# A decoder trunk step: 33 of 44 gate/up pairs by a Strassen scheme, with the residual kept in DRAM meanwhile

## The chip, the cores and the metric

The kernel runs on one core of a Trainium2 chip. TensorE (PE) multiplies, VectorE (DVE), ScalarE (ACT) and GpSimd (POOL) work element by element, and SyncE (SP) issues all DMAs of this kernel, in order. The metric is the device time of one execution in microseconds, the median of three runs. "PEld" in the profile is PE's loading of the stationary operand, which overlaps its matmuls.

## The reference

One inference step of a trunk of two layers, for a prompt of 512 tokens and 8 samples of 8 new tokens, which share all weights: 576 rows of 1024 channels. Cut to what matters:

```python
for i in range(DEPTH):                      # 2
    h = rms_norm(x, norm_mix_pre[i])
    m = pool_mixer(h, ...) if i % 2 == 0 else gdn_mixer(h, ...)   # layer 0: pooling; layer 1: gated delta rule
    x = x + rms_norm(m, norm_mix_post[i])
    h = rms_norm(x, norm_ffn_pre[i])
    x = x + rms_norm(swiglu(h, ffn_w_in[i], ffn_w_out[i]), norm_ffn_post[i])

def swiglu(h, w_in, w_out):                 # w_in (1024, 5632), w_out (2816, 1024)
    gu = h @ w_in
    return (jax.nn.silu(gu[..., :D_FF]) * gu[..., D_FF:]) @ w_out
```

All data are float32. The pooling and the delta rule also return their new states.

## The kernel before

**Layout.** Channels lie on the 128 partitions (8 chunks of 128, index `c` or `k`), the 576 rows along the free dimension, in two halves: half 0 of 256 columns, half 1 of 320 (`HALVES`). Half 0's products go through the ring of three PSUM banks "A", half 1's through the three of "B" (`RING`); "n0" and "n1" are one bank each, for norms and transposes.

**Precision.** Every large product is made of float32 values that are split into a high and a low part: `split2` and `Weights.split` copy on ACT (`wh`, `hH`, `aH`) and subtract on DVE or POOL (`wl`, `hL`, `aL`), and `mm3` sums three matmuls for each chunk of 128 contracted channels: high by high, high by low, low by high.

**Feed-forward layers.** 2816 = 22 x 128, so there are 22 pairs of a gate and an up chunk in a layer. `ffn` lists chunks block by block (`FBLOCKS`, of 8, 7 and 7 pairs): for each pair "g" and "u" (8 x 3 matmuls a half each), then 8 output chunks "y" that contract the block's activations. The first chunks (14 in layer 0, 10 in layer 1) run for half 0 and then again for half 1, so that half 1's norm can be finished beside half 0; then each chunk's weights serve both halves; the last 8 output chunks again run half by half, so that half 0's end (`finish0`, `finish1`) lies beside half 1's products. A weight chunk is 512 KB (`wraw`, three buffers), an output chunk of a 7-pair block 448 KB.

**The end.** In layer 1 the residual is transposed beside the feed-forward work into `xT` (`turn_x`). As each of the last outputs `y` comes, `turn_y` scales it and PE transposes it into banks of the other half's ring, one bank for each row piece and four channel chunks; `finish1` then makes the row norms and adds.

**The mixer of layer 1.** The delta rule's first half of the output product is parked in DRAM (`y_d`), its result `og_d` too, and the residual since the end of layer 0 (`x_d`). When the mixer's pools are closed, `y_d` and `x_d` are loaded, and the second half of the output product is added to it by DVE.

**What sets the order.** Nearly all instructions are recorded by `Plan.put`, and issued by `Plan.finish` in an order that a list scheduler chooses: forward passes with estimated durations, in-order engines and the operations' dependences; 40 rounds with randomly stirred priorities; the best is kept. So all of them have the same line, 283 (302 in the change). An operation of `EITHER` may go to DVE or POOL. Where the planner sees PE waiting for long, it puts idle matmuls there (`ps_w<-ones`, line 279; 298 in the change), whose results nobody reads.

Of the kernel before, what the change touches and what calls it, by code (L numbers as in the profile page):

```python
# [20 lines left out]
P = 128  # L21
# [7 lines left out]
HALVES = ((0, 256), (256, 320))  # L29
DFF = 2816  # L30
FBLOCKS = (8, 7, 7)
# [19 lines left out]
class Plan:  # L51
# [22 lines left out]
    def start(self):  # L74
        self.on = True
        self.ops, self.last, self.tags = [], {}, {}
        self.gone, self.ends, self.home, self.after = set(), set(), {}, {}
        self.banks, self.holds = {}, {}

# [57 lines left out]
    @staticmethod  # L137
    def rows(ap):

        n = list(ap.ap)[0][1]  # L140
        return 32 if n <= 32 else 64 if n <= 64 else 128
# [46 lines left out]
    def put(self, method, calls, a, k):  # L188
# [6 lines left out]
        preds = set()  # L195
# [3 lines left out]
        for x, write in [(x, False) for x in ins] + [(x, True) for x in outs]:  # L199
# [5 lines left out]
            log = self.last.setdefault(name, [])  # L205
# [6 lines left out]
            if x.space == SB and (write or not log):  # L212
                preds.update(self.after[self.home[name]])
            if t.tag in self.tags:
# [3 lines left out]
                if write and p >= bufs:  # L218
                    preds.update(q[0] for q, _ in self.last[names[p - bufs]])
            for q, w in log:  # L220
                if (write or w) and q[0] != i and self.meet(r, q[1]):
                    preds.add(q[0])
            log.append(((i, r), write))
# [18 lines left out]
    def close(self, *pools):  # L242

        self.gone |= {t for t, home in self.home.items() if home in pools}
        touched = {q[0] for t in self.gone for q, _ in self.last[t]}
# [253 lines left out]
def hybrid_kernel(  # L499
# [55 lines left out]
    hv = [None, None]  # L555

    def new_h(hi):
        hv[hi] = [hp.tile([P, NC, HALVES[hi][1]], F32R, name="h%s%d" % (x, hi), tag="h%s%d" % (x, hi), bufs=1)
                  for x in "HL"]

    for hi in range(2):
        new_h(hi)
# [4 lines left out]
    y_d = [dp.tile([P, NC, n], F32, name="y_d%d" % o0) for o0, n in HALVES]  # L567
# [105 lines left out]
    def h_of(hi):  # L673
        hi_, lo = hv[hi]
        return lambda k: (hi_[:, k], lo[:, k])
# [6 lines left out]
    def halftile(tp, what, hi, bufs, shape=None):  # L682
        n = HALVES[hi][1]
        return tp.tile(list(shape or (P, n)), F32, name=what, tag="%s%d" % (what, hi), bufs=bufs)

    def add_sq(tp, acc, src, c, hi):

        if c == 0:
            acc.append(halftile(tp, "nacc", hi, 1))
            ACT.activation(acc[0], src, AF.Square)  # L690
        else:
            sq = halftile(tp, "nsq", hi, 2)
# [14 lines left out]
    def rstd(tp, acc, hi, on_dve=False):  # L707

        n = HALVES[hi][1]
        offs = [0, P] if n == 256 else [0, P, n - P]  # L710
        ps = bank("n%d" % hi)
# [3 lines left out]
        rc = halftile(tp, "nrc", hi, 1, (P, 4))[:, :len(offs)]  # L715
        if on_dve:

            v, t = (halftile(tp, w, hi, 1, (P, 4))[:, :len(offs)] for w in ("nv", "nt"))
# [5 lines left out]
        dg = halftile(tp, "ndg", hi, 1)  # L724
        DVE.tensor_tensor(dg[:, :256].rearrange("p (i t) -> p i t", i=2), ident.unsqueeze(1).to_broadcast([P, 2, P]),
                          rc[:, :2].unsqueeze(2).to_broadcast([P, 2, P]), op=mult)
        if n > 256:
            DVE.tensor_scalar(dg[:, 256:], ident[:, SMP:], rc[:, 2:3], None, op0=mult)
        pr = bank("n%d" % hi)[:, :n]
# [3 lines left out]
    def post_norm(tp, x, m, acc, hi, gpost, acc2, add_eng=(POOL,), on_dve=False):  # L733

        o0, n = HALVES[hi]
        r = rstd(tp, acc, hi, on_dve)
        for c in range(NC):
            mc = m[o0][:, c]
            xc = x[:, c, o0:o0 + n]
# [3 lines left out]
            if acc2 is not None:  # L743
                add_sq(tp, acc2, xc, c, hi)

    def pre_norm(tp, x, acc, hi, gpre, on_dve=False):
        o0, n = HALVES[hi]
        r = rstd(tp, acc, hi, on_dve)
        for c in range(NC):
            t = halftile(tp, "nh", hi, 2)  # L750
            DVE.scalar_tensor_tensor(out=t, in0=x[:, c, o0:o0 + n], scalar=prm[:, gpre + c:gpre + c + 1],
                                     in1=r, op0=mult, op1=mult)
            split2(t, hv[hi][0][:, c], hv[hi][1][:, c])

    def post_pre(tp, x, m, acc, hi, gpost, gpre, fast=False):
        acc2 = []
        post_norm(tp, x, m, acc, hi, gpost, acc2, (DVE, POOL) if fast else (POOL,), hi == 1)
        pre_norm(tp, x, acc2, hi, gpre, hi == 1)


    def ffn(layer, y, wts, ap_, tp, head, tail, finish, beside=None, turn=None):
# [3 lines left out]
        chunks = []  # L765
        f0 = 0
        for bi, nb in enumerate(FBLOCKS):
            for f in range(nb):
                chunks.append(("g", bi, f, f0, nb))
                chunks.append(("u", bi, f, f0, nb))  # L770
            for m in range(NC):
                chunks.append(("y", bi, m, f0, nb))
            f0 += nb
        state = [dict(acts={}, acc=None, turn=None) for _ in HALVES]

        def load(i, eng=EITHER):
            kind, bi, j, f0, nb = chunks[i]
            if kind == "y":
                return wts.load(wout, f0 * P, j * P, nb, eng=eng)
            return wts.load(win, 0, (0 if kind == "g" else DFF) + (f0 + j) * P, NC, eng=eng)  # L780

        def run(i, hi, w):
            kind, bi, j, f0, nb = chunks[i]
            o0, n = HALVES[hi]
            s = state[hi]
            ps = bank("AB"[hi])[:, :n]
            if kind != "y":
                mm3(ps, w, h_of(hi), NC)
                if kind == "g":
                    sg = halftile(ap_, "sg", hi, 2)  # L790
                    ACT.activation(sg, ps, AF.Silu)
                    s["sg"] = sg
                else:
# [1014 lines left out]
```

## Time and profile before

| | |
|---|---|
| runs | 1635.97, 1636.36, 1646.14 us; median 1636.36 |
| profiled execution | span 1636.5 us |
| PE / PEld / DVE / ACT / POOL busy | 1590.0 / 1533.0 / 983.8 / 699.4 / 115.4 us |
| chain that ended last | PE 34% of the span, DVE 3%, DMA 2%, ACT 1% |
| granted PE clock, mean | 0.986 |
| HBM | 161.93 MB read, 25.80 MB written |

A row of groups reads: line, engine, operation, output<-inputs, shape, count, then total busy time, mean of one in ns, the idle time of the engine before them and what ended it. The busy time of PE counts a matmul from its start to a modelled end, and neighbouring matmuls overlap. The stages in time: the pooling mixer until about 60 us, layer 0's feed-forward until about 490, the delta-rule mixer until about 1190, layer 1's feed-forward until the end.

### The profile page before, as it was taken

How to read it: one execution, taken by the hardware profiler on the slowest of the kernel's cores; microseconds unless marked ns; L12 is line 12 of the kernel's file. 1: busy time of each engine (PE TensorE's matmuls, PEld its weight loads, DVE VectorE, ACT ScalarE, POOL GpSimd, SP SyncE). 2: the span in 40 equal slices, each digit the busy share in tenths (PEclk: the TensorE clock that was granted, in tenths of full speed). 3: DMA queues.
4: the chain of work that ended last, by engine and by line, in shares of the span. 5: the costliest groups of instructions: out<-in, count | busy, mean ns of one | idle time of the engine just before them, and what ended most of it. 6: DMA issues, size and time to landing. Idle time of an engine off the chain costs nothing. (4 is left out here: it accounts for less than half of the span.)

```text
span 1636.5 us, 30622 instructions
## 1 busy us (share of the span) xinstructions
PE 1590.0 (97%) x12287; PEld 1533.0 (94%) x12287; DVE 983.8 (60%) x2049; ACT 699.4 (43%) x1528; POOL 115.4 (7%) x254
## 2 busy tenths in 40 slices
PE   8999999999999999998999999799999999999998
PEld 8999999999999998888889898699999999999997
DVE  6883222233387798996998999547794312233245
ACT  7653322223355956453553463324464222222244
POOL 4100000000001011020221120000000000000000
PEclk9999999999999999999999999899999999999998
DMA  6354232232366433424335343457644332223333
GB/s 177 104 153 131 79 90 87 68 91 79 97 173 171 119 107 91 140 63 127 103 89 140 98 115 119 143 162 230 191 143 135 97 90 79 73 77 94 91 102 115
DMA packets 339853, 189.49 MB, mean 116 GB/s; under 512 B 13047, under 2 KB 334368, under 8 KB 339447
## 3 DMA queue, kind: packets, MB, share of 16 engines
q1 hardware_dynamic: 339711, 187.53, 39.6%
q8 instruction: 97, 1.59, 0.4%
q14 instruction: 45, 0.37, 0.1%
HBM read 161.93 MB, written 25.80 MB: 115 GB/s over the span
## 5 line engine op out<-in xcount | busy, mean ns | idle before, releaser
L283 ACT ACTIVATE wh<-wraw 128x1024 fp32r<-128x1024 f32 (+2 forms) x259 | 267.7, 1035 | 488.6 <-PE ps_A L283 222.1
L283 DVE TENSOR_TENSOR wl<-wraw,wh 128x1024 fp32r<-128x1024 f32 (+2 forms) x252 | 299.1, 1192 | 271.8 <-PE ps_A L283 86.8
L283 PE MATMUL ps_m<-hH,wh 128*128 128x320 f32 (+1 forms) x832 | 245.9, 312 | 4.3 <-ACT u L283 2.1
L283 PE MATMUL ps_m<-hH,wl 128*128 128x320 f32 (+1 forms) x832 | 244.6, 311 | 0.0
L283 PE MATMUL ps_m<-hL,wh 128*128 128x320 f32 (+1 forms) x832 | 243.1, 309 | 0.1
L283 PE MATMUL ps_B<-hL,wh 128*128 128x320 f32 x768 | 218.8, 311 | 0.1
L283 PE MATMUL ps_B<-hH,wh 128*128 128x320 f32 x768 | 218.8, 311 | 0.0
L283 PE MATMUL ps_B<-hH,wl 128*128 128x320 f32 x768 | 218.5, 311 | 0.3 <-DVE wl L283 0.2
L283 PE MATMUL ps_A<-hH,wh 128*128 128x256 f32 x768 | 205.2, 283 | 1.4 <-DVE yo L283 1.4
L283 PE MATMUL ps_A<-hH,wl 128*128 128x256 f32 x768 | 205.0, 283 | 0.0
L283 PE MATMUL ps_A<-hL,wh 128*128 128x256 f32 x768 | 204.9, 283 | 0.0
L283 PEld LDWEIGHTS ps_m<-hH,wh 128*128 128x128 f32 x832 | 155.4, 192 | 9.2 <-ACT u L283 3.4
L283 PEld LDWEIGHTS ps_m<-hL,wh 128*128 128x128 f32 x832 | 155.8, 193 | 3.1 <-issue 1.6
L283 PEld LDWEIGHTS ps_m<-hH,wl 128*128 128x128 f32 x832 | 155.5, 193 | 2.8 <-issue 1.3
L283 PEld LDWEIGHTS ps_A<-hH,wh 128*128 128x128 f32 x768 | 142.1, 190 | 2.1 <-issue 1.6
L283 PEld LDWEIGHTS ps_A<-hH,wl 128*128 128x128 f32 x768 | 142.3, 190 | 0.1
L283 PEld LDWEIGHTS ps_A<-hL,wh 128*128 128x128 f32 x768 | 141.9, 190 | 0.2
L283 PEld LDWEIGHTS ps_B<-hL,wh 128*128 128x128 f32 x768 | 139.6, 189 | 0.6 <-DVE hL L283 0.4
L283 PEld LDWEIGHTS ps_B<-hH,wl 128*128 128x128 f32 x768 | 139.2, 189 | 0.8 <-DVE wl L283 0.7
L283 PEld LDWEIGHTS ps_B<-hH,wh 128*128 128x128 f32 x768 | 139.4, 189 | 0.3 <-ACT hH L283 0.2
L283 PE MATMUL ps_B<-aH,wl 128*128 128x320 f32 x352 | 100.8, 311 | 0.0
L283 PE MATMUL ps_B<-aH,wh 128*128 128x320 f32 x352 | 100.8, 310 | 0.0
(383 smaller groups left out, 2994.2 us busy)
## 6 DMA issues: line engine op xcount, KB each, us to landing
wraw<-in_ffn_w_in_dram SPq DMA_DIRECT2D x112, 512.0 KB
wraw<-in_gdn_w_in_dram SPq DMA_DIRECT2D x56, 512.0 KB
wraw<-in_ffn_w_out_dram SPq DMA_DIRECT2D x48, 448.0 KB
wraw<-in_gdn_w_out_dram SPq DMA_DIRECT2D x24, 512.0 KB
wraw<-in_ffn_w_out_dram SPq DMA_DIRECT2D x16, 512.0 KB
St<-in_state_gdn_rec_dram SPq DMA_DIRECT2D x32, 256.0 KB
out_dram<-St SPq DMA_DIRECT2D x32, 256.0 KB
z_d<-zz SPq DMA_DIRECT2D x16, 288.0 KB
```

The lines of the kernel that those rows point to most:

```text
L283: calls[e](*a, **k)
```

## The change

**The scheme.** For 16 pairs of layer 0 and 17 of layer 1, the chunk's gate and up columns are treated as one matrix product of 2 x 2 blocks: the contracted channels in two halves of 4 chunks (`KQ`), the rows in two halves of 288 (`EVEN`), gate and up as the two columns. Seven half-size products (`product`, each 4 x 3 matmuls of 288 columns) replace eight. The sums of the inputs are made once a layer (`sums`, in place in `y`, which holds the normed input by then; `t1` to `t4`, split into `ta`, `tb` and a part of `hH`, `hL`), those of the weights for each pair (`load`: `s1raw`, `graw`, `wraw` in place, high and low parts `s1h`/`s1l`, `dh`/`dl`, `wh`/`wl`). The sums of the results are partly made by going on in the same bank: `pa` takes four products and is read by ACT after each of the first three, `pc` takes two and is read by DVE between them. Pairs use the A and the B ring in turn.

**The head and the blocks.** The other 6 and 5 pairs, at the head of a layer, run as before, half by half. The blocks are 6, 5, 4, 7 and 5, 5, 5, 7 pairs; the output products have 288 columns for both halves.

**The residual.** `ta` takes the residual's memory (tag "x"). In layer 0 the residual is written to `x_m` and loaded again (`back`) for the layer's end; in layer 1 it is transposed piece by piece into `x_t` in DRAM and loaded as `xa`, `xb` (`back_x`). Row pieces at the end follow the even halves: three for each half (`PIECES`), where there were two and three.

**The mixer's output.** `y_d` and `x_d` come back in pieces of one chunk of a half, each held behind an earlier product (`plan.behind`). `hH` and `hL` are one tile each instead of one for each half, and the planner's bookkeeping tells reads from writes. The core of the diff:

```diff
-HALVES = ((0, 256), (256, 320))
+HALVES = (Half(0, 0, 256), Half(1, 256, 320))
+EVEN = (Half(0, 0, 288), Half(1, 288, 288))
+PIECES = (((0, 128), (128, 128), (256, 32)), ((288, 128), (416, 96), (512, 64)))
-FBLOCKS = (8, 7, 7)
+FBLOCKS = ((6, 5, 4, 7), (5, 5, 5, 7))
...
+    class Strassen:
+        def __init__(self, xp, ap_, tp, wts, xtag):
+            self.ta = xp.tile([P, 4, KQ, EV], F32R, name="ta", tag=xtag, bufs=1)
+            self.tb = ap_.tile([P, 2, KQ, EV], F32R, name="tb", tag="tb", bufs=1)
+        def sums(self, y):
+            x11, x12, x21, x22 = (y[:, k:k + KQ, o:o + EV] for k in (0, KQ) for o in (0, EV))
+            EITHER.tensor_tensor(x11, x11, x12, op=sub)
+            EITHER.tensor_tensor(x12, x22, x12, op=sub)
+            DVE.scalar_tensor_tensor(out=x22, in0=x11, scalar=-1.0, in1=x22, op0=mult, op1=sub)
+            DVE.scalar_tensor_tensor(out=x21, in0=x22, scalar=-1.0, in1=x21, op0=mult, op1=sub)
...
+                split2(src, h, l)
...
+        def load(self, src, cols):
+            g = ap_.tile([P, 8, P], F32, name="graw", tag="graw", bufs=2)
+            u = w.p.tile([P, 8, P], F32, name="wraw", tag="wraw", bufs=w.raw)
+            for t, col in zip((g, u), cols):
+                SP.dma_start(t, src[:, col:col + P].rearrange("(k p) m -> p k m", p=P))
...
+            EITHER.tensor_tensor(s1, u[:, lo], u[:, up], op=add)
+            EITHER.tensor_tensor(u[:, lo], u[:, lo], g[:, lo], op=add)
+            a = w.split(g)
...
+            split2(s1, *s)
+            EITHER.tensor_tensor(g[:, lo], s1, g[:, lo], op=add)
+            EITHER.tensor_tensor(g[:, up], g[:, lo], g[:, up], op=add)
...
+            split2(g, *b)
+            c = w.split(u)
...
+        def product(self, ps, wt, xt, first=False):
+            (wh, wl), (xh, xl) = wt, self.acts[xt]
+            for k in range(KQ):
+                for i, (w, v) in enumerate(((wh, xh), (wh, xl), (wl, xh))):
+                    PE.matmul(ps, w[:, k], v[:, k], start=first and k + i == 0, stop=k == KQ - 1 and i == 2,
+                              skip_group_check=not first)
+        def gated(self, w, tag, act):
+            pa, pb, pc = (bank(tag)[:, :EV] for _ in range(3))
...
+            self.product(pa, w["g1"], "x11", True)
+            ACT.activation(p1, pa, AF.Copy)
+            self.product(pb, w["g2"], "x21", True)
+            DVE.tensor_tensor(g[:, 0], pb, p1, op=add)
+            self.product(pa, w["s2"], "t2")
+            ACT.activation(n2, pa, AF.Copy)
+            self.product(pc, w["s1"], "t1", True)
+            self.product(pa, w["s3"], "t3")
+            ACT.activation(n3, pa, AF.Copy)
+            DVE.tensor_tensor(n3, pc, n3, op=add)
+            self.product(pc, w["s4"], "x22")
+            DVE.tensor_tensor(g[:, 1], pc, n2, op=add)
+            self.product(pa, w["u2"], "t4")
+            ACT.activation(g, g, AF.Silu)
+            for i, u in enumerate((pa, n3)):
+                DVE.scalar_tensor_tensor(out=g[:, i], in0=u, scalar=-1.0, in1=g[:, i], op0=mult, op1=mult)
+            split2(g.rearrange("p i t -> p (i t)"), *act)
...
+                SP.dma_start(x_m[:, :, o0:o0 + n], x[:, :, o0:o0 + n])
...
+                if not back:
+                    back.append(xp.tile([P, NC, T], F32, name="xb", tag="x", bufs=1))
+                    for h in EVEN:
+                        SP.dma_start(back[0][:, :, h.o:h.o + h.n], x_m[:, :, h.o:h.o + h.n])
...
-    for hi, (o0, n) in enumerate(HALVES):
-        SP.dma_start(y[o0], y_d[hi])
...
+            if len(past) > 1:
+                plan.behind(past[-2])
+            SP.dma_start(yc, y_d[hi][m])
```

What this makes of the order, at three places. First SP's queue at the delta-rule mixer's output, before (`yo` is the parked half of the product, `x` the residual):

```order
L283 DMA og<-og_d 128x320
L283 DMA wraw<-in_gdn_w_out_dram 128x8x128 x3
L283 DMA yo_2748<-y_d_105 128x2048
L283 DMA yo_2749<-y_d_106 128x2560
L283 DMA x_2750<-x_d 128x8x256
L283 DMA x_2750<-x_d 128x8x320
L283 DMA wraw<-in_gdn_w_out_dram 128x8x128 x8
```

and in the change:

```order
L302 DMA wraw<-in_gdn_w_out_dram 128x8x128 x2
L302 DMA yo<-y_d_105 128x256 x2
L302 DMA wraw<-in_gdn_w_out_dram 128x8x128 x2
L302 DMA yo<-y_d_105 128x256 x2
L302 DMA wraw<-in_gdn_w_out_dram 128x8x128 x2
L302 DMA yo<-y_d_105 128x256
L302 DMA x_2813<-x_d 128x256 x2
L302 DMA yo<-y_d_105 128x256
L302 DMA x_2813<-x_d 128x256 x2
```

Four loads of 1 to 1.3 MB have become 32 loads of one chunk, spread among the weights.

Second, PE inside a Strassen pair of layer 0's last block (`ps_B_1039` is its `pc`, `ps_B_1037` its `pb`, `ps_A_1012` the pair before):

```order
L302 MATMUL ps_A_1012<-hL_98,wh_1009 128x288
L302 MATMUL ps_B_1039<-ta_506,s1l_1029 128x288
L302 MATMUL ps_B_1037<-hH_97,wh_1026 128x288
L302 MATMUL ps_A_1012<-hH_97,wl_1010 128x288
L302 MATMUL ps_B_1037<-hL_98,wh_1026 128x288
L302 MATMUL ps_B_1037<-hH_97,wl_1027 128x288
L302 MATMUL ps_B_1037<-hH_97,wh_1026 128x288
L302 MATMUL ps_B_1037<-hL_98,wh_1026 128x288
L302 MATMUL ps_B_1039<-hH_97,dh_1030 128x288
```

Between the last matmul of `pc`'s first product (`s1l`) and the first of its second (`dh`), DVE reads the bank; six matmuls into other banks stand there.

Third, PE at the switch from half 0 to half 1 in layer 1's last block, before (`nh` is a scaled output chunk, transposed into the B banks; `ps_n0` the row norms; `aH`, `aL` the activations of half 1's first output product):

```order
L283 MATMUL ps_B_3572<-ident_68,nh_3575 128x128
L283 MATMUL ps_B_3574<-ident_68,nh_3575 128x128
L283 MATMUL ps_n0_3591<-ones_73,nsq_3588 128x1
L283 MATMUL ps_n0_3591<-ones_73,nacc_3529 128x1
L283 MATMUL ps_n0_3591<-ones_73,nsq_3588 128x1
L283 MATMUL ps_B_3572<-ident_68,nh_3582 128x128
L283 MATMUL ps_B_3574<-ident_68,nh_3582 128x128
L283 MATMUL ps_B_3597<-aH_3402,wh_3594 128x320
L283 MATMUL ps_B_3597<-aL_3403,wh_3594 128x320
```

and in the change:

```order
L302 MATMUL ps_n0_3750<-ones_73,nsq_3745 32x1
L302 MATMUL ps_B_3727<-ident_68,nh_3739 128x128
L302 MATMUL ps_B_3731<-ident_68,nh_3739 32x128
L302 MATMUL ps_B_3729<-ident_68,nh_3739 128x128
L302 MATMUL ps_B_3727<-ident_68,nh_3746 128x128
L302 MATMUL ps_B_3729<-ident_68,nh_3746 128x128
L302 MATMUL ps_B_3731<-ident_68,nh_3746 32x128
L298 MATMUL ps_w_3822<-ones_73 128x128 x4
L302 MATMUL ps_B_3756<-aH_3516,wh_3753 128x288
L302 MATMUL ps_B_3756<-aL_3517,wh_3753 128x288
```

Half 0's transposes stand in two B banks before and in three in the change; half 1's first product, which began among them, now stands behind the last of them and four fillers.

More of the change, by code (lines that the diff above doesn't have):

```diff
@@ L78, in start, with behind @@
         self.banks, self.holds = {}, {}
+        self.extra = set()
+    def behind(self, ap):
+        if self.on:
+            self.extra = {q for old in self.last[ap.tensor.name] for q, _ in old}
     class Engine:
@@ L135, in meet, with within @@
         return a[0] < b[1] and b[0] < a[1] and a[2] & b[2] != 0
+    @staticmethod
+    def within(a, b):
+        return b[0] <= a[0] and a[1] <= b[1] and a[2] & ~b[2] == 0
     @staticmethod
@@ L211, in put @@
             assert name not in self.gone, name
-            if x.space == SB and (write or not log):
+            if x.space == SB and (write or not (writes or reads)):
                 preds.update(self.after[self.home[name]])
@@ L218, in put @@
                 if write and p >= bufs:
[L219 to L223, printed above, removed]
+                    for old in self.last[names[p - bufs]]:
+                        preds.update(q for q, _ in old)
+            for old in (writes, reads) if write else (writes,):
+                preds.update(q for q, at in old if q != i and self.meet(r, at))
+            if write:
+                for old in (writes, reads):
+                    old[:] = [(q, at) for q, at in old if q == i or not self.within(at, r)]
+            (writes if write else reads).append((i, r))
         work = mode = 0
@@ L244, in close @@
         self.gone |= {t for t, home in self.home.items() if home in pools}
-        touched = {q[0] for t in self.gone for q, _ in self.last[t]}
+        touched = {q for t in self.gone for old in self.last[t] for q, _ in old}
         later = {j for i in touched for j in self.ops[i][4]}
@@ L1759, in finish1 @@
+        def finish1(hf, acc):
+            if not xT:
+                back_x()
+            ps = bank("n%d" % hf.i)
+            rc = halftile(tp, "nrc", hf, 1, (P, 4))
+            last = PIECES[hf.i][2][1]
+            for i, (o, n) in enumerate(PIECES[hf.i]):
+                n = n if i == 2 else P
                 for k, a in enumerate(acc):
-                    PE.matmul(ps[:n, i:i + 1], a[:, tt * P - o0:tt * P - o0 + n], ones[:, 0:1],
+                    PE.matmul(ps[:n, i:i + 1], a[:, i * P:i * P + n] if i < 2 else a[:, EV - n:], ones[:, 0:1],
@@ L1775, in hybrid_kernel @@
-        ffn(1, y, wts, ap_, tp, 10, NC, finish1, turn_x(), turn_y)
+            for r, q in ((slice(0, P), slice(0, 2)), (slice(0, last), slice(2, 3))):
+                ACT.activation(rc[r, q], ps[r, q], AF.Sqrt, bias=eps_c[r], scale=1.0 / D)
+                DVE.reciprocal(rc[r, q], rc[r, q])
+            for i, (o, n) in enumerate(PIECES[hf.i]):
+                for k in range(2):
+                    to = xT[o][:, k * 4 * P:(k + 1) * 4 * P]
+                    DVE.scalar_tensor_tensor(out=to, in0=yT[o, k], scalar=rc[:n, i:i + 1], in1=to, op0=mult, op1=add)
+                SP.dma_start(y_prompt[0, o:o + n] if o < SEQ else y_sample.rearrange("b t d -> (b t) d"), xT[o])
@@ L1776, in hybrid_kernel @@
+        ffn(1, x, y, wts, xp, ap_, tp, 5, finish1, turn_x(), turn_y)
     plan.finish()
```

387 lines of the change are left out of this document (197 added, 190 removed).

## Prediction

> **What bounds the kernel now.** I read the page's busy line first, then a table by stage, then the rows of the stages that change.
>
> ```profile
> span 1636.5 us, 30622 instructions
> PE 1590.0 (97%) x12287; PEld 1533.0 (94%) x12287; DVE 983.8 (60%) x2049; ACT 699.4 (43%) x1528; POOL 115.4 (7%) x254
> ```
>
> The three runs have a median of 1636.36 us and the profiled span is 1636.5 us, so nothing worth counting lies around the span, and I work against 1636.5. Busy matmuls overlap, so 97% alone does not say that the array is full. The stages do (us; busy time of PE, of its weight loads, DVE, ACT and POOL, with counts; granted clock; DMA share; GB/s):
>
> ```profile
> 52.00:120.00 68.00, 67.79 (x522) 66.31 (x522) 57.04 (x121) 40.02 (x73) 4.22 (x5) 1.00 0.49 140
> 120.00:460.00 340.00, 340.00 (x2553) 340.00 (x2552) 111.67 (x163) 101.29 (x156) 0.00 (x0) 1.00 0.33 94
> 520.00:1120.00 600.00, 567.85 (x4632) 520.61 (x4631) 495.24 (x1162) 297.28 (x818) 79.16 (x153) 0.97 0.41 116
> 1240.00:1580.00 340.00, 340.00 (x2550) 339.94 (x2549) 103.25 (x150) 93.75 (x151) 0.00 (x0) 1.00 0.30 87
> ```
>
> Rows 2 and 4 are the two feed-forward layers. For 680 us PE never rests, at a granted clock of 1.00, while DVE and ACT work a third of the time. Both rows hold 256- and 320-column matmuls in equal numbers and give the same pace: 340 / 2553 = 0.1332 us each. The change uses 288 columns, the mean of the two, so I price its matmul at 0.1332 us. Row 3 is the delta-rule mixer, where DVE and latency matter too; the change leaves its arithmetic alone.
>
> **Matmuls removed.** An ordinary gate/up pair is 2 x 8 x 3 matmuls for each half, 96 in all. The scheme has 7 products of 4 x 3 = 84, so 12 go for each of 33 pairs: 396 x 0.1332 = **-52.7 us**, all from stages where PE alone sets the time. The output products keep their number. Order's PE total agrees: 11175 matmuls become 10812, which is 396 fewer and 33 more (16 transposes, 11 idle fillers, 6 of the norms).
>
> The Trainium skill, "TensorE: Matmul & The Clock Gate", section "Back-to-back issue gap", gives a sustained stream of weight loads and matmuls 81 ns at 128 columns and 131 ns at 512. Between these, 288 columns would take an estimated 102 ns and the 396 matmuls 40 us. The stage table says 133 ns at the mean of 288, and the measurement decides.
>
> **Work added beside PE.** Rows by shape (busy us, mean ns of one, then idle time):
>
> ```profile
> L283 DVE TENSOR_TENSOR wl<-wraw,wh 128x1024 fp32r<-128x1024 f32 x203 | 246.7, 1221 | 261.6 <-PE ps_A L283 84.5 <-ACT wh L283 55.3 <-issue 42.2
> L283 ACT ACTIVATE wh<-wraw 128x1024 fp32r<-128x1024 f32 x210 | 221.8, 1057 | 396.2 <-PE ps_A L283 161.9 <-PE ps_B L283 81.2 <-issue 68.9
> L283 DVE TENSOR_TENSOR wl<-wraw,wh 128x896 fp32r<-128x896 f32 x48 | 52.0, 1086 | 10.2 <-ACT wh L283 4.2 <-PE ps_B L283 2.4 <-PE ps_A L283 2.4
> L283 DVE TENSOR_TENSOR sg<-sg,ps_B 128x320 f32<-128x320 f32 x44 | 21.4, 485 | 119.2 <-PE ps_B L283 118.1 <-ACT wh L283 0.8
> L283 DVE TENSOR_TENSOR sg<-sg,ps_A 128x256 f32<-128x256 f32 x44 | 18.3, 415 | 53.1 <-PE ps_A L283 52.0 <-ACT wh L283 0.7
> L283 DVE SCALAR_TENSOR_TENSOR nh<-x,prm,ps_n 128x320 f32<-128x320 f32 x24 | 12.1, 539 | 2.8 <-PE ps_n L283 2.8
> L283 DVE SCALAR_TENSOR_TENSOR nh<-x,prm,ps_n 128x256 f32<-128x256 f32 x24 | 10.5, 473 | 0.4 <-PE ps_n L283 0.4
> L283 ACT ACTIVATE sg<-ps_B 128x320 f32<-128x320 f32 x44 | 18.9, 430 | 32.7 <-PE ps_B L283 32.3
> L283 ACT ACTIVATE sg<-ps_A 128x256 f32<-128x256 f32 x44 | 16.6, 378 | 11.0 <-PE ps_A L283 10.9
> ```
>
> DVE's slope is (1221 - 1086) / 128 = 1.055 ns a column, so 512 columns take 0.68 us and 576 take 0.75. A Strassen pair gives DVE three 1024-column subtractions (3.66), five 512-column operations (3.41), three 288-column sums (3 x 0.45), two 288-column multiplications (2 x 0.51) and one 576-column split (0.75): 10.2 us. PE needs 84 x 0.1332 = 11.2. ACT has three and a half weight copies (3.7), three reads of a bank (3 x 0.40) and two passes of 576 columns (some 1.3): 6.2. So PE stays the bound, but DVE's share goes from a third to nine tenths inside a run of pairs; the output products between runs (6.4 us of PE a pair, little DVE) give it air. The sums of the inputs, four of 1152 columns and their splits (some 11 us of DVE a layer), lie beside the first block's output products: 6 or 5 x 48 x 0.1332 = 38 or 32 us of PE whose inputs are ready.
>
> **The hand-offs.** Four times a pair a bank is read out and then accumulated into again, 132 times in all. A round trip is the last matmul (0.28 to 0.31, next fence) plus an ACT read (0.40) and starting gaps, about 0.8 us. In the order at least 6 other matmuls (0.80 us) stand in each, 8 or fewer in a third of them. That just covers it, if ACT or DVE is free when the product ends.
>
> ```profile
> L283 PE MATMUL ps_A<-hH,wh 128*128 128x256 f32 x768 | 205.2, 283 | 1.4 <-DVE yo L283 1.4
> L283 PE MATMUL ps_B<-hH,wh 128*128 128x320 f32 x768 | 218.8, 311 | 0.0
> ```
>
> Bounds: nothing, as in the feed-forward rows today; or all of it exposed, (0.8 - 0.13) x 132 = 88 us. The nearest row is the 340.00 of 340.00, so I take **+3 us** for these waits and DVE's narrow margin together.
>
> **The mixer's output.** Today PE stops there:
>
> ```profile
> 1134.57 0.28 PE L283 MATMUL ps_A<-hH,wl 128*128 128x256 f32 x1
> 1134.69 7.75 PE L279 MATMUL ps_w<-ones 128*128 128x128 f32 x68
> 1143.87 0.36 PE L283 MATMUL ps_A<-hH,wh 128*128 128x256 f32 x1 [1.43 <-DVE yo L283]
> ...
> 1135.32 2.33 SPq L283 DMA_DIRECT2D yo<-y_d  x2
> 1143.31 1.08 DVE L283 TENSOR_TENSOR yo<-yo,ps_A 128x256 f32<-128x256 f32 x3 [4.25 <-DMA yo<-y_d]
> ```
>
> The fillers (ps_w) hide a wait of 9.3 us: three output products are done, and DVE cannot add until all 2.3 MB of partial sums, issued at 1135.3, have landed. The change asks for one 128 KB piece at a time. The issue still waits for the old pools, so 1135.3 stays, and a piece needs some 2 to 3 us. I take **-5 us** (-9 to 0). What is late next is the weights of the following products: on SP's in-order queue they stand behind the pieces, and a piece is now held until the product two before it is done, so a late product would hold the next weights too; with two weights ahead of each pair of pieces (2 x 24 x 0.12 = 5.8 us of PE) I count nothing for that.
>
> **The residual's way back.** In each last block the residual's 2.3 MB stand on SP's queue behind three output weights and ahead of the other 13.
>
> ```profile
> 1135.32 7.91 DMA yo<-y_d
> yo<-y_d SPq DMA_DIRECT2D x1, 1280.0 KB
> yo<-y_d SPq DMA_DIRECT2D x1, 1024.0 KB
> ```
>
> The same bytes took 7.9 us; a 448 KB weight behind them adds 1.5 at that rate and its two passes 2: 11.4 us. PE's cover is 38 matmuls after the scheme's last use of that memory (5.1) and three weights of 21 (8.4): 13.5. Just hidden; I take **+2 us** for both layers (0 to 16). Writing the residual out costs nothing: DMA's share is 0.30 in these stages.
>
> **The switch between the halves at the end.** Half 0 now has three row pieces instead of two, and their transposes fill all three B banks, where half 1's products must go. Order shows those products behind everything. What they wait for took, before:
>
> ```profile
> 1595.79 0.41 DVE L283 TENSOR_TENSOR yo<-yo,ps_A 128x256 f32<-128x256 f32 x1
> 1598.53 1.28 ACT L283 ACT_TABLE_LOAD   x1
> 1599.83 0.26 ACT L283 ACTIVATE nrc<-ps_n,epsd 128x2 f32<-128x2 f32 x1
> 1600.39 0.75 DVE L283 SCALAR_TENSOR_TENSOR xT<-ps_B,nrc,xT 128x512 f32<-128x512 f32 x1
> ...
> 1598.12 6.41 PE ps_B L283 x44
> ```
>
> From the last addition to the first freed bank: 1601.14 - 1595.79 = 5.35 us, during which PE had started on half 1 at 1598.1. Now it cannot: **+5 us** (0 to 7).
>
> **Small ones.** Sixteen more transposes at 7.75 / 68 = 0.114 us: **+1.8**. Layer 0's first half has 12 weight chunks instead of 14, 2 x 24 x 0.12 = 5.8 us less PE work under half 1's norm, in the stretch where DVE is busy 57 of 68 us: **+2** (0 to 5.8). The mixer's order is drawn anew; PE's 600 - 568 = 32 us of rest there may move by a quarter: **0** (-8 to +8).
>
> **Sum.** -52.7 + 3 - 5 + 2 + 5 + 1.8 + 2 = -43.9: 1636.5 - 43.9 = 1592.6, **1593 us**.
>
> **The rivals.** *Half-covered hand-offs or a short DVE.* If a Strassen pair's DVE work runs 15% over (11.7 us), or each hand-off loses 0.12 us, 33 pairs lose 16 us: 1609. For: DVE at 10.2 of 11.2, ACT serving in order with 1.06 us copies in its queue. Against: both layers run today without a gap. 14%.
>
> *Exposed hand-offs, the slower side.* Place: the four reuses of a bank in a pair. If ACT is mostly in the middle of a weight copy when a product ends (1.06 / 2 = 0.53 us), 132 x 0.53 = 70 us: 1663. It decides from 44 / 132 = 0.33 us each. Against: a waiting read stands at the head of its queue. 4%.
>
> *A clock that falls.* Where PE pauses between small products the clock is granted less:
>
> ```profile
> 1020.00:1040.00 20.00, 14.05 (x219) 11.47 (x218) 10.93 (x22) 9.71 (x23) 0.62 (x2) 0.86 0.62 202
> 1040.00:1060.00 20.00, 17.09 (x111) 13.78 (x112) 12.12 (x30) 3.79 (x16) 2.47 (x3) 0.80 0.27 79
> ```
>
> The Strassen products are 33 x 11.2 = 369 us; at 0.86 they would cost 60 us more: 1653. It needs rests of a sixth of the time, which the order does not show. 2%. The Trainium skill states this mechanism in the same page, section "A second HAM failure mode: psum-queue depth-cycling": short rests between groups of matmuls that cycle through banks drop the clock again and again. The 0.93 to 1.00 of all other stages speaks against it here.
>
> *Everything covered.* The last two rises vanish and the new mixer order gains: 1575 to 1581. 9%. That the change saves nothing is excluded by the count of matmuls.
>
> **How the numbers follow.** My forecast (1581 to 1605) has 68%, the rivals 14, 4, 2 and 9%, and 3% is left for a sum of waits that ends between 1620 and 1653. From 1576 to 1616 lie the forecast, most of the covered case and three quarters of the half-covered one: over 8 in 10. One per cent, 16 us, is about what a measurement tells from no change: faster (below 1620) 0.91, within it 0.03, slower 0.06.
>
> **What would show it.** Feed-forward stages with PE busy 100% at 1.00 and 133 ns a 288-column matmul; two stages some 26 us shorter each; DVE up by 33 x (10.2 - 4.2) plus some 34 for the sums and the added block, to about 1215 us (4.2 is today's pair: two 1024-column passes and, for each half, a multiplication and a split of like width, 2 x 1.22 + 2 x 0.49 + 2 x 0.42); a mixer wait of 4 us instead of 9.3; a hole of some 5 us at the last switch. I am wrong if the Strassen stretches show PE waiting on DVE or ACT, or if half 0's weights come late behind the residual.

## The result and the profile after

The changed kernel takes 1594.63 us (median of four, 1590.50 to 1596.57) against 1636.16 before: a ratio of 0.973, 95% interval 0.970 to 0.976. A second measurement gave 1594.32 and again 0.973 (0.971 to 0.975). The forecast was 1593. The profiled execution is the shortest of the four, 1590.50 us with a span of 1588.8, so the two profiled spans (1636.5 before) differ by 47.7 us and the medians by 41.5.

The busy line of the page after:

```profile
span 1588.8 us, 30549 instructions
PE 1543.5 (97%) x11941; PEld 1479.0 (93%) x11941; DVE 1190.6 (75%) x2377; ACT 797.1 (50%) x1654; POOL 120.9 (8%) x257
```

DVE was forecast at 1215 us. The table by stage of the changed kernel (columns as before the change: busy time of PE, weight loads, DVE, ACT and POOL with counts; granted clock; DMA share; GB/s), with the middle of each feed-forward layer in rows 1 and 3:

```profile
140.00:420.00 280.00, 280.00 (x2108) 279.33 (x2107) 186.33 (x288) 124.24 (x190) 0.00 (x0) 1.00 0.33 96
520.00:1100.00 580.00, 552.61 (x4570) 504.80 (x4569) 488.50 (x1161) 292.48 (x806) 70.60 (x142) 0.99 0.41 118
1240.00:1520.00 280.00, 280.00 (x2110) 279.67 (x2109) 189.78 (x290) 126.22 (x193) 0.00 (x0) 1.00 0.33 94
1540.00:1589.00 49.00, 40.16 (x293) 36.98 (x291) 24.92 (x44) 21.59 (x41) 0.00 (x0) 0.90 0.35 109
```

The same two stretches of the kernel before:

```profile
140.00:420.00 280.00, 280.00 (x2099) 280.00 (x2098) 80.81 (x115) 75.57 (x117) 0.00 (x0) 1.00 0.30 86
1240.00:1520.00 280.00, 280.00 (x2094) 279.99 (x2093) 82.99 (x119) 74.41 (x119) 0.00 (x0) 1.00 0.31 90
```

In 280 us PE issues 2108 matmuls where it issued 2099, 0.1328 us each, at a clock of 1.00, although DVE has 2.3 times the work. PE is still the bound in these stretches, and the time went because there are fewer matmuls. Some of DVE's groups in that stretch of the changed kernel:

```profile
L302 DVE TENSOR_TENSOR dl<-graw,dh 128x1024 fp32r<-128x1024 f32 x16 | 19.5, 1222 | 7.8 <-ACT dh L302 7.8
L302 DVE TENSOR_TENSOR s1raw<-wraw 128x512 f32<-128x512 f32 x16 | 11.0, 689 | 6.7 <-DMA wraw<-in_ffn_w_in_dram 6.5
L302 DVE TENSOR_TENSOR y<-y,ps_A 128x288 f32<-128x288 f32 x17 | 7.6, 450 | 11.5 <-PE ps_A L302 11.5
```

With these durations, and 0.75 us for the split of 576 columns, a Strassen pair has 3 x 1.22 + 5 x 0.69 + 3 x 0.45 + 2 x 0.45 + 0.75 = 10.1 us of DVE; the forecast said 10.2.

For the comparison of runs I mark four points in each trace: the first feed-forward matmul, the mixer's first and last product (`ps_m`), and the last instruction of an engine. Layer 0's feed-forward is the column "until the mixer"; layer 1's lies in the last column, behind the mixer's output product. All numbers are us.

| run | start of layer 0's feed-forward | until the mixer | mixer | mixer's last product to the end |
|---|---|---|---|---|
| before | 52.8 | 463.1 | 608.4 | 507.9 |
| changed | 56.9 | 443.6 | 603.7 | 480.4 |
| changed, second measurement | 58.4 | 445.5 | 603.9 | 480.0 |
| one product twice | 54.1 | 470.2 | 610.8 | 503.8 |
| one product left out | 57.8 | 417.2 | 603.5 | 451.7 |
| two more on DVE | 62.2 | 440.0 | 595.1 | 480.7 |
| four more on DVE | 57.7 | 469.5 | 607.6 | 500.3 |
| one ring | 60.6 | 458.3 | 607.3 | 495.4 |
| other seed | 55.3 | 445.4 | 603.0 | 477.2 |
| switch | 59.2 | 443.6 | 605.5 | 475.6 |
| switch and reload | 58.8 | 444.8 | 603.8 | 474.3 |
| shorter heads | 60.1 | 437.8 | 600.8 | 480.2 |
| whole loads | 71.2 | 442.4 | 616.0 | 491.4 |
| pieces in the kernel before | 55.2 | 467.4 | 599.2 | 502.7 |

The two traces of the unedited changed kernel differ by up to 1.9 us in a column, so much is chance. All rows but the first and the last share the mixer's code. It takes 595 to 611 us, and 616 in the trace of whole loads, an execution 14 us above that kernel's median; the mixer of the kernel before goes from 608.4 to 599.2 when its order is drawn anew. That is what an order is worth, and why small terms are read at their place in the trace and not from times.

### The profile page after: what moved, and what is told of

Its sections match the earlier page's. It is cut to its first block, busy times and chain, and to the rows that moved or that the text cites. A ratio compares the mean times of both kernels' runs of the same rounds, so it can differ in the third digit from the quotient of the medians.

```text
span 1588.8 us, 30549 instructions
## 1 busy us (share of the span) xinstructions
PE 1543.5 (97%) x11941; PEld 1479.0 (93%) x11941; DVE 1190.6 (75%) x2377; ACT 797.1 (50%) x1654; POOL 120.9 (8%) x257
## 4 chain that ended last, share of the span: by engine, by line
PE 42%; DVE 16%; ACT 3%; DMA 2%; issue 2%; SPq 0%; POOL 0%; DVEq 0%; ACTq 0%
PE ps_B L302 15%; PE ps_A L302 12%; PE ps_m L302 6%; PE ps_s L302 4%; PE ps_k L302 3%; DVE ac L302 3%; DVE ii L302 2%; DVE ia L302 2%; DVE Uw L302 2%; DVE wl L302 1%; DVE vt L302 1%; PE ps_n L302 1%; DVE QD L302 1%; PE ps_x L302 1%; DVE St L302 1%
## 5 line engine op out<-in xcount | busy, mean ns | idle before, releaser
L302 ACT ACTIVATE wh<-wraw 128x1024 fp32r<-128x1024 f32 (+4 forms) x240 | 233.2, 976 | 246.1 <-PE ps_B L302 89.6
L302 DVE TENSOR_TENSOR wl<-wraw,wh 128x1024 fp32r<-128x1024 f32 (+4 forms) x233 | 259.4, 1118 | 89.9 <-ACT wh L302 42.3
L302 PE MATMUL ps_B<-hH,wl 128*128 128x320 f32 (+1 forms) x444 | 128.9, 305 | 1.0 <-DVE wl L302 1.0
L302 PE MATMUL ps_B<-hH,wh 128*128 128x320 f32 (+1 forms) x444 | 129.3, 304 | 0.0
L302 PE MATMUL ps_B<-hL,wh 128*128 128x320 f32 (+1 forms) x444 | 128.3, 304 | 0.0
L302 PE MATMUL ps_A<-hH,wh 128*128 128x256 f32 (+1 forms) x432 | 121.1, 291 | 0.7 <-DVE yo L302 0.7
L302 PE MATMUL ps_A<-hL,wh 128*128 128x256 f32 (+1 forms) x432 | 120.8, 290 | 0.0
L302 PE MATMUL ps_A<-hH,wl 128*128 128x256 f32 (+1 forms) x432 | 120.0, 290 | 0.1
L302 PE MATMUL ps_B<-aH,wh 128*128 128x288 f32 x352 | 99.3, 296 | 1.2 <-DVE xa L302 1.2
L302 PE MATMUL ps_B<-aL,wh 128*128 128x288 f32 x352 | 99.2, 296 | 0.0
```

The source lines that it names most:

```text
L302: calls[e](*a, **k)
```

## Experiments on the pairs: what bounds them

**One product more, one fewer.** In `gated`:

```
-            self.product(pb, w["g2"], "x21", True)
+            self.product(pb, w["g2"], "x21", True)
+            self.product(pb, w["g2"], "x21", True)
```

> The second product of each of the 33 Strassen pairs is computed twice (the repeat starts its bank anew), so that a pair has 96 matmuls again, as an ordinary pair has, and keeps the scheme's work on DVE and ACT: 396 matmuls more than the changed kernel. If PE alone sets the time of the Strassen stretches, this adds 396 x 0.1332 = 52.7 us to 1594.6: 1647, and the 11 us by which that exceeds the kernel before are what everything but the saved matmuls costs. If hand-offs or DVE hold the pairs up by some 10 us in the changed kernel, the extra product covers that, and the time is near 1637.

and, in another kernel:

```
-            self.product(pc, w["s1"], "t1", True)
...
-            DVE.tensor_tensor(n3, pc, n3, op=add)
-            self.product(pc, w["s4"], "x22")
+            DVE.tensor_tensor(n3, pb, n3, op=add)
+            self.product(pc, w["s4"], "x22", True)
```

> The product of s1 with t1 is left out of each Strassen pair, and the sum that used it reads another bank, so that DVE and ACT do the same work: 72 matmuls a pair, 396 fewer than the changed kernel. If PE alone set the time there would be 52.7 us less: 1542. By my account DVE's 10.2 us a pair then exceed PE's 9.6 inside a run of pairs; with two pairs' weights prepared ahead, three of five pairs lose 0.6 us: 33 x 0.6 x 0.6 = 12 us, 1554. If DVE limited the pairs already, the time would stay near 1595.

Measured: 1648.3 us (ratio to before 1.005, 1.003 to 1.007) and 1536.1 us (0.935, 0.933 to 0.937). The two feed-forward columns together rise by 26.6 + 23.4 = 50.0 us with the product more and fall by 26.4 + 28.7 = 55.1 with the product fewer, around 52.7. Time follows the count of matmuls in both directions. With six products (which also take one of the four hand-offs of a pair away, that on `pc`) DVE's account, 10.1 us, is larger than PE's inside a run of pairs, 9.6. Still nothing is lost: from 140 to 400 us PE is busy for 260.00 of 260 us. So the 12 us that I expected there did not come. With as many matmuls in a pair as before, the rest of the change leaves the kernel 0.5% slower.

Between these two kernels lie 792 matmuls of 288 columns and 470.2 + 503.8 - 417.2 - 451.7 = 105.1 us of feed-forward, 0.1327 each. The Trainium skill, "TensorE: Matmul & The Clock Gate", section "Back-to-back issue gap", would give an estimated 102 ns at this width (on a line between its 81 ns at 128 columns and 131 ns at 512). These runs do not agree, and the measured 133 ns decide.

**More work on DVE.** In `load`, subtractions are repeated, two in one kernel, and the same two lines twice in the other:

```
             c = w.split(u)
+            DVE.tensor_tensor(b[1], g, b[0].bitcast(F32), op=sub)
+            DVE.tensor_tensor(c[1], u, c[0].bitcast(F32), op=sub)
```

> Each Strassen pair makes two of its 1024-column subtractions twice on DVE: 2 x 1.22 = 2.4 us more, 12.6 us a pair against PE's 11.2 inside a run of pairs, and still under the 17.6 us of PE that a pair and its share of output products take. If only the mean over a block counts, nothing is lost: 1595. If a run of pairs counts, with two pairs prepared ahead, three of five pairs lose 1.4 us: 33 x 0.6 x 1.4 = 28 us, 1622. If DVE is already the limit, all of it comes on top: 33 x 2.4 = 80 us, 1675.

> Four 1024-column subtractions more on DVE in each Strassen pair: 4.9 us, 15.1 a pair. A block of five pairs then gives DVE 5 x 15.1 plus some 13 us for its output products, 89 us, against PE's 5 x 17.6 = 88. If the mean over a block counts, as two more subtractions at no cost suggest, the break is just here: 1595 to 1605. If a run of pairs counted after all and two more were just covered, three of five pairs lose 3.9 us: 33 x 0.6 x 3.9 = 77 us, 1672.

Measured: 1589.2 us with two (0.967, 0.965 to 0.970), nothing lost; 1637.8 with four (0.9985, 0.997 to 0.9999), so the whole gain is gone. The tables by stage, with a slice of 20 us below; first two more:

```profile
140.00:420.00 280.00, 279.15 (x2101) 278.77 (x2100) 219.02 (x316) 123.00 (x189) 0.00 (x0) 1.00 0.31 90
1480.00:1500.00 20.00, 20.00 (x153) 20.00 (x152) 20.00 (x28) 8.34 (x14) 0.00 (x0) 1.00 0.35 100
```

and four more:

```profile
140.00:420.00 280.00, 276.69 (x2047) 272.08 (x2047) 232.48 (x320) 114.54 (x174) 0.00 (x0) 1.00 0.29 85
220.00:240.00 20.00, 19.32 (x141) 18.38 (x141) 20.00 (x28) 8.06 (x13) 0.00 (x0) 1.00 0.25 70
```

With two more, DVE is full for 20 us on end and PE does not notice; I take it that prepared weights and the output products between the runs carry it over. With four more a full slice leaves PE 141 matmuls of 153, though DVE's mean over the stretch is only 232 / 280 = 83%. From 180 to 420 us, the seven slices of 20 us in which DVE is full have 141 to 149 matmuls, the five others 152 or 153. So neither of my two accounts was right: the break lies between 12.6 and 15.1 us a pair, above PE's 11.2 inside a run and below the 17.6 of a pair with its output products. The loss of 25.9 + 19.9 = 46 us in the feed-forward columns is 1.4 a pair; if all beyond the break is lost, which no run tests, the break is at an estimated 15.1 - 1.4 = 13.7.

PE's waits hardly point at the preparation of weights. I call the time from the start of one matmul to the start of the next a step, idle fillers left out; a streaming step is 0.133 us. In the two stretches of 300 us from 140 and from 1240, PE's steps are 39 us longer than streaming with four more subtractions. Of these, 12.1 us end with `nh`, ACT's read of a bank, 7.2 with DVE's sums of results (`sgg`, `nsq`), and only 3.2 with DVE's weight halves (`wl`, `dl`). My reading is that PE, short of prepared weights, has too few other products to put between a bank's last matmul and its next.

PE's busy time hides most of the loss: 276.69 of 280, while the count of matmuls is down by 2.9%. The Trainium skill, "Perfetto Trace Analysis", section "Identifying the Most-Contended Engine", says that matmul busy time is a poor measure of how near a kernel is to its limit, and that the work done and the busy share of the weight loads should be read instead. The row agrees: PEld goes from 279.33 to 272.08, 2.6% less.

**The hand-offs.** A tight one in the timeline of the changed kernel: the last matmul of `s2`'s product on `ps_A`, and the first of `s3`'s on the same bank (start, duration in us):

```profile
223.94 0.29 PE L302 MATMUL ps_A<-ta,dl 128*128 128x288 f32 x1
224.07 0.30 PE L302 MATMUL ps_B<-hH,dh 128*128 128x288 f32 x1
...
224.73 0.30 PE L302 MATMUL ps_B<-hH,dl 128*128 128x288 f32 x1
224.87 0.43 PE L302 MATMUL ps_A<-tb,wh 128*128 128x288 f32 x2
```

and ACT's read between them:

```profile
224.27 0.41 ACT L302 ACTIVATE nh<-ps_A 128x288 f32<-128x288 f32 x1 [1.18 <-PE ps_A L302]
```

The round trip is 0.93 us: 0.33 from the start of the last matmul to the start of the read, 0.41 for the read, 0.19 until the next matmul starts. PE's seven steps in it (six other matmuls stand between the two) take 7 x 0.133 = 0.93: it streams on. Of the 33 hand-offs from `s2` to `s3`, eleven have only six matmuls between them; ten of these take 0.91 to 0.94 us, one 1.02. On `pc` three of 33 have six, and take 0.93. What covers them shows when the cover is taken away:

```
-                    fast.gated(fast.load(win, (f * P, DFF + f * P)), "AB"[f % 2], acts[f])
+                    fast.gated(fast.load(win, (f * P, DFF + f * P)), "A", acts[f])
```

> All Strassen pairs use the three A banks instead of the A and the B ring in turn, so that two neighbouring pairs can't lie beside each other in time. Within one pair every reuse of a bank but one has another product of 12 matmuls (1.6 us) to cover it; the sum that frees pc needs the third read of pa, so the last products wait once a pair for ACT and DVE. If it is the second ring that covers the hand-offs (0.8 us each, one or two a pair left bare, 0.67 us net), this costs 33 x 0.67 to 33 x 1.3 = 22 to 44 us: 1617 to 1638. If the hand-offs are free in any order, because output products fill in, the time stays at 1594.

Measured: 1626.5 us (0.991, 0.989 to 0.994), 32 above the changed kernel. Its table by stage has fewer matmuls, at full clock:

```profile
140.00:420.00 280.00, 276.68 (x2054) 273.09 (x2053) 177.87 (x275) 117.69 (x178) 0.00 (x0) 1.00 0.31 88
1240.00:1520.00 280.00, 277.40 (x2054) 273.74 (x2053) 178.14 (x270) 122.11 (x185) 0.00 (x0) 1.00 0.34 98
```

In the two stretches of 300 us from 140 and from 1240, PE's steps are 29.5 us longer than streaming (5.5 in the changed kernel). Of these, 17.9 end with `nh` at 17 places: the read of `g1`'s product at 16, of `s2`'s at one. One of the 16, PE and then ACT:

```profile
227.04 0.30 PE L302 MATMUL ps_A<-ta,s1l 128*128 128x288 f32 x1
227.17 0.38 PE L298 MATMUL ps_w<-ones 128*128 128x128 f32 x2
227.85 0.54 PE L302 MATMUL ps_A<-ta,dh 128*128 128x288 f32 x2 [0.29 <-ACT nh L302]
```

```profile
226.44 1.06 ACT L302 ACTIVATE wh<-wraw 128x1024 fp32r<-128x1024 f32 x1 [0.66 <-PE ps_A L302]
227.41 0.39 ACT L302 ACTIVATE nh<-ps_A 128x288 f32<-128x288 f32 x1
```

The read stands behind a weight copy of 1.06 us on ACT, and so it does at all 16 places. This is the mechanism of the rival that I gave 4%. It is real, some 1 us a time, and in the changed kernel no step inside the pairs ends that way: the second ring hides it. I had expected the bare hand-off at `pc`; the size came out within the range, the place did not. The other 11.6 us end at many places and were not followed up.

## Experiments on the edges

**The changed kernel again**, unedited, beside three of the kernels below:

> The changed kernel once more, beside the next three on the same chip: 1594.6 us, or the same ratio of 0.973 to the kernel before if this chip is a little slower or faster.

Measured: 1594.3 us, 0.973 (0.971 to 0.975). The trials of the switch, of whole loads and of the reload are held against this.

**The order alone.** The planner's `SEED` is 3 instead of 2.

> Only the seed of the planner's stirred priorities is another, so that all instructions are the same and the order is drawn anew. My prediction allowed 8 us either way for that: 1587 to 1603, and I expect the feed-forward stretches to keep their lengths within 2 us and the delta-rule mixer to carry most of the difference. If the order were worth more than that, single terms of a few us could not be told from times at all.

Measured: 1590.1 us (0.968, 0.966 to 0.971). The feed-forward columns move by +1.8 and -3.2 us where I expected 2 at most, and the mixer, which was to carry most of it, by -0.7. The draw is worth up to half a per cent.

**The mixer's output.** In the changed kernel PE's wait there is short:

```profile
1113.44 0.28 PE L302 MATMUL ps_A<-hH,wl 128*128 128x256 f32 x1
1113.56 1.27 PE L298 MATMUL ps_w<-ones 128*128 128x128 f32 x10
1115.51 0.36 PE L302 MATMUL ps_A<-hH,wh 128*128 128x256 f32 x1 [0.68 <-DVE yo L302]
```

From start to start PE waits 2.1 us instead of 9.3. The load of the first pieces, as SP issues them and as the chain of work shows them from the issue on:

```profile
1110.15 1.81 SPq L302 DMA_DIRECT2D yo<-y_d  x2
1110.15 4.60 DMA yo<-y_d
```

One kernel takes the pieces back and loads `y_d` and then `x_d` whole:

> The partial sums and the residual at the end of the delta-rule mixer are loaded whole again, as in the kernel before; everything else as in the changed kernel, with the order drawn anew. If the pieces are what shortened the wait from 9.3 to 2.1 us, it comes back: 7 us at that place, 1602 with the mixer's order worth a few us either way (the other seed moved the whole by less than 8). If the shorter wait came from another place of the issue in the new order, the wait stays near 2 us.

Measured: 1612.7 us (0.985, 0.982 to 0.988); its profiled execution took 1626.7, of which 13 us lie ahead of the feed-forward, so its trace is read at this place alone:

```profile
1139.30 2.62 PE L298 MATMUL ps_w<-ones 128*128 128x128 f32 x22
1143.73 0.36 PE L302 MATMUL ps_A<-hH,wh 128*128 128x256 f32 x1 [1.81 <-DVE yo L302]
...
1149.55 8.87 PE L298 MATMUL ps_w<-ones 128*128 128x128 f32 x78
1158.17 0.36 PE L302 MATMUL ps_A<-hH,wh 128*128 128x256 f32 x1
```

There are two waits, of 4.6 and 8.7 us from start to start. The second is my own doing: the kernel before issued `x_d` half by half after three products, and I put all 2.3 MB of it ahead of the weights on SP's queue:

```profile
1134.23 3.99 SPq L302 DMA_DIRECT2D yo<-y_d  x2
1138.27 1.89 SPq L302 DMA_DIRECT2D x<-x_d  x1
1140.21 19.27 SPq L302 DMA_DIRECT2D wraw<-in_gdn_w_out_dram  x6
```

The weights then come late, and ACT waits for them before it copies:

```profile
1153.72 1.06 ACT L302 ACTIVATE wh<-wraw 128x1024 fp32r<-128x1024 f32 x1 [3.10 <-DMA wraw<-in_gdn_w_out_dram]
```

DVE's half of these weights takes 1.23 us from 1154.81, so both halves are there at 1156.04. Of the 8.7 us some 6.6 are therefore late weights, and the last 2.1 are fillers, which the planner put there and which last longer than needed. So this run says more than it was asked: the place in the queue matters beside the size of the pieces. A cleaner trial is the kernel before with the pieces alone (its order, too, is drawn anew):

```
-                SP.dma_start(x[:, :, o0:o0 + n], x_d[:, :, o0:o0 + n])
+            if len(past) > 1:
+                plan.behind(past[-2])
+            SP.dma_start(yc, y_d[hi][m])
...
+            if m >= 4:
+                for c in (2 * m - 8, 2 * m - 7):
+                    plan.behind(ps)
+                    SP.dma_start(x[:, c, o0:o0 + n], x_d[:, c, o0:o0 + n])
```

> The kernel before with one part of the change alone: the partial sums at the end of the delta-rule mixer, and the residual behind them, are loaded in pieces held behind the products, as the change does it. If the pieces shorten the wait by themselves, PE's wait of 9.3 us there becomes about 2: 1636 - 7 = 1629, with the redrawn order worth up to 8 us either way, so the wait in the trace decides. If the wait stays near 9, the change owes its shorter wait to its own order.

Measured: 1633.7 us (0.996, 0.994 to 0.998). The wait is 4.0 us, taken from start to start as the 9.3 were:

```profile
1131.33 0.40 PE L288 MATMUL ps_A<-hH,wl 128*128 128x256 f32 x2
1131.57 2.84 PE L284 MATMUL ps_w<-ones 128*128 128x128 f32 x24
1135.45 0.35 PE L288 MATMUL ps_A<-hH,wh 128*128 128x256 f32 x1 [1.04 <-DVE yo L288]
```

```profile
1131.33 3.46 DMA yo<-y_d
```

The wait is 5.3 us shorter, where I expected 7, and the last column with it (507.9 to 502.7). That the time falls by a similar 4.9 says less, since layer 0's column is 4.3 longer and the mixer 9.2 shorter by the new order.

The traces tell what the waits are made of. Counted from the mixer's last product, the first load of `y_d` is issued after 11.0 us in the kernel before, 9.1 in this one and 5.9 in the changed kernel; the load that PE's chain waits for lands 7.9, 3.5 and 4.6 us after its issue. So the changed kernel owes 3.3 us of its shorter wait to the pieces and 5.0 to the earlier issue, less 1.0 because PE also runs out of products 1.0 us earlier: 7.2. The forecast had the issue where it was and 2 to 3 us for a piece, so its -5 came near by two errors that partly cancel. Over the eleven traces of the changed mixer with pieces, the issue comes after 3.4 to 8.8 us and the wait is at most 4.3, and 0.8 where the issue is earliest; with whole loads and the issue after 4.6 us it is 4.6. That settles the 1.9 us between this trial and the changed kernel: they lie within what the order alone does.

**The switch.** Where half 0's transposes hold the B banks, the changed kernel shows PE with fillers and transposes only:

```profile
1545.33 0.49 PE L302 MATMUL ps_B<-ident,nh 128*128 128x128 f32 x3
1545.65 1.50 PE L298 MATMUL ps_w<-ones 128*128 128x128 f32 x12
1547.60 0.33 PE L302 MATMUL ps_B<-ident,nh 128*128 128x128 f32 x1 [0.44 <-ACT yT L302]
...
1550.76 1.06 PE L298 MATMUL ps_w<-ones 128*128 128x128 f32 x8
1553.02 0.40 PE L302 MATMUL ps_B<-aH,wh 128*128 128x288 f32 x1 [1.20 <-DVE xa L302]
```

The edit, in `out` and in `turn_y`:

```
-            ps = bank("AB"[hf.i])[:, :hf.n]
+            ps = bank("A" if turn is not None and bi == len(blocks) - 1 else "AB"[hf.i])[:, :hf.n]
...
-                    yT[o, c // 4] = bank("BA"[hf.i], (P, 4, P))...
+                    yT[o, c // 4] = bank("B", (P, 4, P))...
```

> In layer 1's last block the output products of both halves go through the three A banks and the transposes of both through the three B banks; the order of everything ahead of that block stays. If the hole at the switch comes from half 1's products waiting for the B banks that half 0's transposes hold, products can run on and the two gaps there (2.05 and 2.37 us) go: 4.4 us less than the changed kernel, ratio to it 0.997. If the hole is the latency of half 0's norm itself, it moves to half 1's transposes and the time stays.

Measured: 1589.4 us (0.969, 0.967 to 0.971), 4.9 under the changed kernel on the same chip. The slice of 20 us, before this edit and with it:

```profile
1540.00:1560.00 20.00, 18.30 (x141) 17.20 (x140) 11.15 (x20) 10.58 (x18) 0.00 (x0) 1.00 0.51 161
```

```profile
1540.00:1560.00 20.00, 20.00 (x156) 19.92 (x155) 11.49 (x18) 13.28 (x24) 0.00 (x0) 1.00 0.56 159
```

Both gaps are gone. The hole was made by banks, not by the norm's latency. No other kernel of this study that computes the whole result is faster than this one by more than its measurement can tell.

**The residual's way back.** In layer 0's last block of the changed kernel, SP and then PE:

```profile
410.44 1.30 SPq L302 DMA_DIRECT2D xb<-x_m  x2
412.42 15.73 SPq L302 DMA_DIRECT2D wraw<-in_ffn_w_out_dram  x5
```

```profile
423.66 1.50 PE L298 MATMUL ps_w<-ones 128*128 128x128 f32 x12
425.68 0.40 PE L302 MATMUL ps_A<-aH,wh 128*128 128x288 f32 x1 [0.53 <-ACT wh L302]
```

This gap and the next, 2.16 and 0.89 us from start to start, cost 2.8 beyond two streaming steps. With the switch as above, each half's residual is held back until that half's third output product:

```
+                        if m == 2:
+                            back(hf, state[hf.i]["ps"])
```

> As the run that changes the switch, and in both last blocks each half's residual is loaded when the third output product of that half is done, so that more weights stand ahead of it on SP's queue. If the gaps in the last blocks (2.16 and 0.89 us above streaming in layer 0, some 1.5 in layer 1) are weights that stand behind 2.3 MB of residual, 3 to 4.5 us go besides the 4.4 of the switch: 1586. If the held issue makes the weights behind it late instead, as much is lost there.

Measured: 1590.2 us (0.970, 0.967 to 0.972), no better than the switch alone. The gaps in layer 0's last block are gone, and the loss has moved to the edge to the mixer (two slices of this kernel; the kernel with the switch alone has 148 matmuls and a clock of 1.00 in the second):

```profile
420.00:440.00 20.00, 20.00 (x152) 20.00 (x152) 11.45 (x19) 9.60 (x14) 0.00 (x0) 1.00 0.69 204
462.00:482.00 20.00, 18.99 (x139) 18.08 (x138) 19.03 (x42) 11.78 (x23) 3.36 (x6) 0.91 0.64 184
```

PE waits up to 2.5 us for half 1's norm there, whose residual comes later now, and the clock is granted at 0.91. The held issue only moved the wait, as the last sentence of the expectation feared.

**Shorter heads.** The switch, `FBLOCKS = ((5, 5, 5, 7), (4, 5, 6, 7))` and heads of 5 and 4.

> The switch as in the run before, and heads of 5 and 4 pairs instead of 6 and 5, with blocks of 5, 5, 5, 7 and 4, 5, 6, 7 pairs: two more pairs by the scheme, 24 matmuls fewer, 24 x 0.1332 = 3.2 us. If the shorter heads still cover the second half's norm, 1589.4 - 3.2 = 1586. If they don't, each lost head pair takes 2 x 24 x 0.12 = 5.8 us of PE work from under the norm: up to 11.6 us back, 1598.

Measured: 1589.9 us (0.970, 0.968 to 0.972), the same as without. Layer 0's column falls by 5.8 us and the last one rises by 4.6. In layer 1, PE now waits for half 1's norm:

```profile
1186.18 1.06 PE L298 MATMUL ps_w<-ones 128*128 128x128 f32 x8
1188.50 0.57 PE L302 MATMUL ps_B<-hH,wh 128*128 128x320 f32 x2 [1.26 <-ACT hH L302]
```

The wait shown is 2.4 us from start to start. Between 1140 and 1240 all waits come to 5.0 us above streaming, against 1.4 with heads of six and five: four head pairs no longer cover the norm, five do. The last column is 6.2 us worse than the count of matmuls says; the 2.6 beyond these 3.6 were not found. Layer 0's fall exceeds the 1.6 us of its 12 matmuls; whether the rest is the order drawn anew, this run does not tell.

## Why the prediction was right, by its own steps

The forecast was made of few large and several small terms. What they measured:

| step | forecast | measured |
|---|---|---|
| 396 matmuls | -52.7 | -50.0 and -55.1 by the two trials with one product more and one fewer |
| hand-offs and DVE's margin | +3 | 0: no gap in the Strassen stretches; PE 280.00 of 280 |
| mixer output | -5 | -7.2, by landing -3.3, by the earlier issue -5.0, by PE stopping earlier +1.0 |
| residual's reload, both layers | +2 | +2.8 in layer 0, 0.4 to 0.8 in layer 1 |
| switch | +5 | +4.2 in gaps; 4.9 with the edit that removes it |
| transposes | +1.8 | not separated |
| shorter head | +2 | some +1 in layer 0: gaps above streaming between 70 and 140 us are 2.1, and 1.0 before |
| mixer's order | 0 (-8 to +8) | -4.7; over the runs -13.3 to +2.4, and +7.6 in the trace of whole loads |

The table of marks has +4.1 - 19.5 - 4.7 - 27.5, which is -47.6 between the two profiled executions. Two stretches had no term. The pooling mixer ends 4.1 us later (52.8 to 56.9; 54 to 62 in the other runs, 71 in the slow execution of whole loads): its order was drawn anew as well, and I allowed for that only in the delta-rule mixer. And PE waits 1.9 us more at the edge from layer 0 to the mixer (1.45 and 0.73 us from start to start at 466 and 469), where weights and half 1's norm share DVE, busy for all of the 20 us from 460; I gave that edge no term. These 6.0 us stand against 9.9: the 3 for hand-offs that weren't needed, the 2.2 more at the mixer's output and the 4.7 of a kinder order. So the traces differ by 3.8 us more than the forecast of 43.9, and the medians by 2.4 less. That 1593 lies within 2 us of the measured median is in part luck; the large term and its mechanism are not.

The step with the weakest reasoning was DVE's margin. I compared 10.2 with 11.2 us inside a run of pairs and priced a shortfall from there; the first rival (1609) rests on it, "if a Strassen pair's DVE work runs 15% over". With 12.6 us, 24% over, nothing is lost, so that rival's threshold was far too low. The second rival's mechanism exists and costs about 1 us a time when one ring is left; in the order as it is, it does not occur. My range for the mixer's order was too narrow: the other drawings went to -13.3 us. The third rival, a falling clock, did not come in the pairs: 1.00 in all slices from 140 to 420 and from 1240 to 1520, and 1.00 too with a single ring and its gaps of 1 us. The Trainium skill, "TensorE: Matmul & The Clock Gate", section "A second HAM failure mode: psum-queue depth-cycling", reports a kernel whose clock drops again and again because of short rests between groups of matmuls that cycle through banks. The pairs of these runs do not show it. At the edge to the mixer the clock did fall, to 0.91, in the slice of the switch and reload with a wait of 2.5 us. The range held because the large term was a count times a duration from a stage where PE never rests.

## What to carry to other kernels

Where a stage showed PE at 100% at full clock, removing matmuls paid in full here, as long as the work put beside them kept two things: some other product between the last matmul on a bank and the next one there (here six matmuls, 0.93 us), and prepared operands ahead of PE. A supporting engine may run over PE's pace for tens of us if stages with air follow, but its mean over the layer is no safe bound; look at slices, and at counts of matmuls rather than PE's busy time. When one engine is short, PE's waits may end at other work. In a change of this kind the small losses sit at the edges: find which banks, which place in a DMA queue and which norm stand there, and check that a wait that is removed doesn't come back at the next edge.

## What the runs showed that I had not expected

A shortage on DVE that costs 46 us leaves PE's busy share where it was: 97% of the span in both kernels. DVE full for 20 us on end cost nothing with two more subtractions a pair, and 8% of the matmuls (141 of 153) with four. A load of 2.3 MB put ahead of weights in an in-order queue cost PE 8.7 us at one place, some 6.6 of them by late weights. And of the 7.2 us that the change took off the wait there, more came from an earlier issue than from the smaller pieces.
